# The last three output blocks of each stage run by token parts, with the next stage's first weights loaded ahead of them

## The chip, the cores and the metric

One core of a Trainium2 chip runs the whole program in one launch. The metric is the device time of one execution in microseconds (us). The core has a matrix engine (TensorE, PE in the rows), a vector engine (VectorE, DVE), an activation engine (ScalarE, ACT), GpSimd (POOL), and SyncE (SP), whose queue issues nearly all loads. Data lies in SBUF; matmuls write to eight banks of PSUM.

## The reference, cut to what matters

Two layers work on 512 latent tokens (x) and 256 context tokens (cx), of width 1024:

```
h  = rms_norm(x, norm_attn_w) * (1 + sc_m) + sh_m         # the same for cx, with its own sc and sh
u  = h @ w_in ; ya, yb, yg = three kinds of mixers of u
x  = x + g_m * (concat(ya, yb, yg) @ w_out)
hf = rms_norm(x, norm_ffn_w) * (1 + sc_f) + sh_f
x  = x + g_f * ((silu(hf @ w_gate) * (hf @ w_up)) @ w_down)
...
return rms_norm(x, final_norm_w)
```

The second layer updates no context tokens behind its mixers. What matters here is the place where one product ends and the next begins: each rms_norm needs the sum of squares over all 1024 channels of a token, thus over the outputs of all eight column blocks of the product before it, and the first matmul of the next product needs the normalised h.

## The kernel before, in words

**Layout.** x is kept with channels on the partitions, as eight blocks xT[d] of 128 channels by 768 tokens (layer 0) or 512 (behind the mixers of layer 1). A product is made block by block, d = 0 to 7: `load_w` (L341) brings the weights of one block into a raw tile `wr`, ScalarE rounds them to a high half (`wh`, L345), VectorE subtracts for the low half (`wl`, L346). `proj_ws` (L349) then makes, for each of 4, 7 or 8 blocks of the contraction, three matmuls (high by high, high by low, low by high) per token segment of at most 512 columns. `residual` (L1158) adds the block to xT[d] on VectorE (L1162), squares it on ScalarE (L1173) and adds the square to `acc` (tile MC) on VectorE (L1175).

**Rings.** Tiles of one name rotate over few buffers: `wr` has 2, `wh` and `wl` 3 each, `vh` and `vl` (a second pair for weights, used in the mixers and not in the products at stake) 2 each, and in PSUM `S` has 2 of two banks each, `PT` 2 and `sm` 2 of one bank each. A `wr` buffer is free again when both halves are made.

**The end of a stage.** `tail_blocks` (L1188) makes the last two blocks, d = 6 and 7, by token parts: 512 and 256 tokens in layer 0, twice 256 in layer 1. The order is block 6 and block 7 for part 0, block 6 for part 1, then `token_sums` (L1178) of part 0, block 7 for part 1, the spread of part 0's row, and the sums and the spread of part 1. The sums are matmuls of one column against `ones`: one group over `acc` and one over the squares of block 7. VectorE adds the two (L1207, L1208), GpSimd raises to the power of -0.5 (L286), and three small VectorE instructions refine it (L291, L292, L294). `spread` (L311) lays the row over all partitions by matmuls (L315), and ScalarE copies it from PSUM to SBUF (L320). `make_h` (L323) then makes h for each of the eight blocks d of a part: on VectorE x times scale times row (L336) or, for d = 2, 4 and 6, on ScalarE and GpSimd (L333, L334); the high half on ScalarE (L338, tiles HY and HS) and the low half on VectorE (L339, tiles HZ, PHA and PHB).

There are four such ends, called **end 1** (w_out of layer 0, 4 contraction blocks), **end 2** (w_down of layer 0, its last group of 7), **end 3** (w_out of layer 1) and **end 4** (w_down of layer 1, behind which `final`, L1260, transposes x, scales it by the row and stores it).

**The start of the next stage** uses two weight blocks at once, gate and up (L1290) or the first two of w_in (L559), and multiplies part 0 through all of h before part 1. Their loads stand behind `tail_blocks` in program order.

**Modulation.** In the feed-forward of layer 0 the generator `md` runs 56 steps of `mod_dots` (L234). Each takes one `wr` buffer, loads 512 KB into it and makes four VectorE products (L245). One or two steps are taken in the block loop, and what is left is run off ahead of end 2 (L1327).

**Order.** The program is written as one list; the order on each engine is drawn up ahead of time by a planner with estimated durations, in which the earlier entry of the list goes first where both are ready, and the engines keep to it. `issue_after` puts an instruction behind another one on its engine.

Of the kernel before, what the change touches and what calls it, by code (L numbers as in the profile page):

```python
# [14 lines left out]
P = 128  # L15
# [13 lines left out]
def hybrid_kernel(ctx: ExitStack, tc: tile.TileContext, a, out, dbg=None):  # L29
# [281 lines left out]
    def spread(rstd, n):  # L311

        pb = ps_sm()
        for tb in range(n // P):
            PE.matmul(  # L315
                pb[:, tb * P : (tb + 1) * P], lhsT=rstd[:, tb : tb + 1].to_broadcast([P, P]),
                rhs=ident, start=True, stop=True,
            )
        pbs = T(sb, "pr", 3, [P, NX])[:, 0:n]
        S.activation(pbs, pb[:, 0:n], AF.Copy)  # L320
        return pbs

    def make_h(l, xT, h, pbs, part, shi, sc):  # L323
# [3 lines left out]
        for d in range(KB):  # L327
            aside = d in (2, 4, 6)
            t1 = (mb if aside else ma)([P, NX])[:, 0:n]
            hi, lo = h[0][d][:, c0:c1], h[1][d][:, c0:c1]  # L330
            s_ = sc[d // 4][:, d % 4, v : v + 1]
            if aside:
                S.activation(t1, xT[d][:, c0:c1], AF.Copy, scale=s_)  # L333
                G.tensor_tensor(out=t1, in0=t1, in1=pbs, op=ALU.mult)  # L334
            else:
                V.scalar_tensor_tensor(t1, xT[d][:, c0:c1], s_, pbs, ALU.mult, ALU.mult)  # L336
            sh = mod_ap(l, shi, d, v)
            S.activation(hi, t1, AF.Identity, bias=sh)  # L338
            V.scalar_tensor_tensor(lo, t1, sh, hi.bitcast(F32), ALU.add, ALU.subtract)  # L339
# [176 lines left out]

    for l in range(L):
# [41 lines left out]
        ws = [wblk(i) for i in range(2)]  # L559
# [618 lines left out]
        def token_sums(src, n):  # L1178
            pq = ps_sm()
            for tb in range(n):  # L1180
                ins = PE.matmul(
                    pq[:, tb : tb + 1], lhsT=src[:, tb * P : (tb + 1) * P], rhs=ones[:, 0:1], start=True, stop=True
                )
            return pq[:, 0:n], ins.ins

        fin = False

        def tail_blocks(load, nk, xh, xl, which, order, then):  # L1188

            d0, d1 = KB - 2, KB - 1  # L1190
            ws = [load(d) for d in (d0, d1)]
            pts = [ps_s() for _ in ws]
            rs = []
            ins = None
# [6 lines left out]
            def sums(part, sq):  # L1201
                _, c0, c1 = part
                n = (c1 - c0) // P
                qa, _ = token_sums(acc[:, c0:c1], n)
                qs, ins = token_sums(sq, n)
                va, v = tiny(n), tiny(n)
                V.tensor_scalar(out=va, in0=qa, scalar1=1.0 / D, scalar2=EPS, op0=ALU.mult, op1=ALU.add)  # L1207
                V.scalar_tensor_tensor(v, qs, 1.0 / D, va, ALU.mult, ALU.add)  # L1208
                return rsqrt(v, n), ins
# [30 lines left out]
        for d in range(KB - 2):  # L1240
# [11 lines left out]

        tail_blocks(load_wo, 4, ysh, ysl_, 2, None, norm2)
# [3 lines left out]
        def load_gu(name, j):  # L1257
            return load_w(a[name][l, j].rearrange("p k c -> p (k c)"), 1024)
# [27 lines left out]
        for gi, ng in enumerate(groups):  # L1286
            gh, gl_ = [], []
            for j in range(j0, j0 + ng):
                if j == 0:
                    ws = [load_gu(n, 0) for n in ("w_gate", "w_up")]  # L1290
# [30 lines left out]
            for d in range(KB - 2 if fin else KB):  # L1321
# [97 lines left out]
```

## Time and profile before

| | |
|---|---|
| time, median of 3 runs | 1792.51 us (1790.63 to 1794.35) |
| the profiled execution: time, span | 1792.03 us, 1790.3 us |
| TensorE busy | 1735.2 us, 97% of the span |
| VectorE, ScalarE, GpSimd busy | 1025.0, 623.6, 265.6 us |
| mean granted TensorE clock | 0.986 of full |
| end 1, end 2, end 3 (about) | 482 to 515, 1040 to 1088, 1401 to 1424 us |

Times in rows are microseconds from the start of the span. A timeline's row is the start, the time from the first start to the last end, the engine, the line and the instruction, with the tile written and those read, and how many were merged (x); in brackets is the idle time of the engine ahead of it and what ended it. A merged row's time overlaps the next row's on TensorE, so lengths of matmul work are taken from start to start.

### The profile page before, as it was taken

The page shows a single profiled execution, that of the slowest core. Times are in us where ns is not written, and L with a number is a line of the kernel's source. Part 1 is how long each engine was busy: PE and PEld are TensorE (multiplying, and loading weights), DVE is VectorE, ACT ScalarE, POOL GpSimd, SP SyncE. Part 2 cuts the span into 40 slices and gives each one's busy share as a digit, 9 for nine tenths or more (in the row PEclk, how much of TensorE's full clock was granted, in tenths as well). Part 3 has the DMA queues.
Part 4 walks back from the last instruction along what each step waited for, and adds up shares of the span by engine and source line. Part 5 has one row for each costly group of instructions (what it writes and reads, how often), then busy time and mean ns, then how long its engine had stood idle before and what let it go on. Part 6 is the DMA issues. An engine that isn't in the chain of part 4 may idle for free.

```text
span 1790.3 us, 26514 instructions
## 1 busy us (share of the span) xinstructions
PE 1735.2 (97%) x10290; PEld 1472.0 (82%) x10290; DVE 1025.0 (57%) x2117; ACT 623.6 (35%) x1202; POOL 265.6 (15%) x289
## 2 busy tenths in 40 slices
PE   7999998999999999999999989999999999999998
PEld 3898886778878888888888878998777888888887
DVE  3645557985575455535554575586895743333335
ACT  4422425665352211221122234334655532232222
POOL 0103116652010000000000011222652100000000
PEclk9999998999989999999999999999999999999999
DMA  9744455522223443333343455233722233333332
GB/s 361 250 130 138 167 159 143 138 89 69 74 86 117 123 121 107 118 105 111 125 122 114 122 162 188 74 108 112 198 63 71 83 107 102 98 93 96 99 106 79
DMA packets 93742, 220.61 MB, mean 123 GB/s; under 512 B 18352, under 2 KB 26160, under 8 KB 93616
## 3 DMA queue, kind: packets, MB, share of 16 engines
q1 hardware_dynamic: 77520, 203.60, 37.3%
q10 hardware_dynamic: 16096, 15.31, 2.6%
q8 instruction: 81, 1.33, 0.3%
q14 instruction: 45, 0.37, 0.1%
HBM read 197.44 MB, written 21.43 MB: 122 GB/s over the span
## 4 chain that ended last, share of the span: by engine, by line
PE 87%; DVE 6%; DMA 3%; ACT 2%; issue 1%; POOL 1%; SPq 0%; ACTq 0%; DVEq 0%; POOLq 0%
PE S L357 66%; PE sm L371 3%; PE PT L371 3%; PE sm L459 2%; PE PT L447 2%; PE PT L357 1%; DMA wr<-in_mod_wT_dram 1%; PE S L411 1%; DVE wh L924 1%; PE S L188 1%; PE S L414 1%; PE PT L188 1%; PE PT L990 1%; PE sm L945 1%; PE sm L946 1%
## 5 line engine op out<-in xcount | busy, mean ns | idle before, releaser
L345 ACT ACTIVATE wh<-wr 128x1024 fp32r<-128x1024 f32 (+2 forms) x204 | 198.0, 972 | 742.6 <-PE S L357 567.0
L346 DVE TENSOR_TENSOR wl<-wr,wh 128x1024 fp32r<-128x1024 f32 (+2 forms) x204 | 227.9, 1118 | 186.4 <-ACT wh L345 184.1
L357 PE MATMUL S<-HY,wh 128*128 128x512 f32 (+1 forms) x716 | 215.9, 359 | 3.9 <-ACT HY L338 3.9
L357 PE MATMUL S<-HY,wl 128*128 128x512 f32 (+1 forms) x716 | 212.5, 354 | 0.3 <-DVE wl L346 0.3
L357 PE MATMUL S<-HZ,wh 128*128 128x512 f32 (+1 forms) x716 | 212.1, 354 | 0.6 <-DVE HZ L339 0.6
L357 PE MATMUL S<-HS,wh 128*128 128x512 f32 (+1 forms) x716 | 211.3, 353 | 0.0
L357 PE MATMUL S<-HS,wl 128*128 128x512 f32 (+1 forms) x716 | 209.3, 350 | 0.0
L286 POOL TENSOR_TENSOR tiny<-tiny,mhalf 128x2 f32<-128x2 f32 (+2 forms) x17 | 27.0, 1590 | 1069.6 <-DVE tiny L1208 1020.6
L245 DVE CUSTOM_DVE_ANT_0 PT<-wr,XFB 128x512 f32<-128x512 f32 x112 | 75.6, 715 | 182.8 <-DMA wr<-in_mod_wT_dram 182.8
L357 PEld LDWEIGHTS S<-HY,wh 128*128 128x128 f32 x716 | 118.7, 191 | 24.0 <-ACT HY L338 4.2
L357 PEld LDWEIGHTS S<-HZ,wh 128*128 128x128 f32 x716 | 118.7, 190 | 22.8 <-DVE HZ L339 2.1
L357 PEld LDWEIGHTS S<-HY,wl 128*128 128x128 f32 x716 | 117.8, 190 | 19.7 <-DVE wl L346 0.6
L357 PEld LDWEIGHTS S<-HS,wh 128*128 128x128 f32 x716 | 116.9, 188 | 18.1
L357 PEld LDWEIGHTS S<-HS,wl 128*128 128x128 f32 x716 | 116.2, 188 | 18.9
L357 PE MATMUL S<-PHA,wh 128*128 128x512 f32 (+1 forms) x358 | 105.6, 352 | 0.0
L357 PE MATMUL S<-PHB,wh 128*128 128x512 f32 (+1 forms) x358 | 104.7, 350 | 0.0
L357 PE MATMUL S<-GX,wh 128*128 128x512 f32 (+1 forms) x400 | 97.7, 350 | 0.4 <-DVE KA L1162 0.4
L437 POOL TENSOR_SCALAR pr<-pr,tiny 128x640 f32<-128x640 f32 (+2 forms) x80 | 72.7, 911 | 98.5 <-DVE tiny L435 89.5
L1309 DVE TENSOR_TENSOR MB<-S,MA 128x768 f32<-128x768 f32 (+1 forms) x42 | 34.6, 824 | 72.0 <-PE S L357 72.0
L357 PEld LDWEIGHTS S<-GX,wh 128*128 128x128 f32 x400 | 65.9, 189 | 11.2 <-DVE KA L1162 0.8
L447 PE MATMUL PT<-c,pr 128*128 128x128 f32 x384 | 65.4, 285 | 9.5 <-POOL pr L437 4.5
L431 ACT ACTIVATE pr<-S,tiny 128x640 f32<-128x640 f32 (+2 forms) x80 | 61.5, 770 | 32.6 <-DVE tiny L424 21.2
(436 smaller groups left out, 3670.1 us busy)
## 6 DMA issues: line engine op xcount, KB each, us to landing
wr<-in_mod_wT_dram SPq DMA_DIRECT2D x56, 512.0 KB, 3.8
wr<-in_w_gate_dram SPq DMA_DIRECT2D x44, 512.0 KB, 3.6
wr<-in_w_up_dram SPq DMA_DIRECT2D x44, 512.0 KB, 3.6
wr<-in_w_blk_dram SPq DMA_DIRECT2D x28, 512.0 KB, 3.8
wr<-in_w_down_dram SPq DMA_DIRECT2D x32, 448.0 KB, 3.4
wr<-in_w_out_dram SPq DMA_DIRECT2D x32, 256.0 KB, 2.8
wr<-in_w_down_dram SPq DMA_DIRECT2D x16, 512.0 KB, 3.5
QN<-in_mod_w_dram SPq DMA_DIRECT2D x24, 256.0 KB, 5.3
```

The lines of the kernel that those rows point to most:

```text
L188: PE.matmul(pm[32 * j : 32 * j + 32, 0:512], lhsT=cs[:, k, :], rhs=w[k], start=(k < 4), stop=(k >= 4), tile_position=(0, 32 * j),)
L245: V.tensor_tensor_reduce(out=ptile() if v == 0 else wv, in0=wv, in1=rows[2 * v + hf], scale=1.0, scalar=0.0, op0=ALU.mult, op1=ALU.add, ac ...
L286: POW.tensor_tensor(out=y, in0=v, in1=mhalf[:, 0:n], op=ALU.pow)
L345: S.activation(hi, raw, AF.Copy)
L346: V.tensor_tensor(lo, raw, hi.bitcast(F32), ALU.subtract)
L357: ins = PE.matmul(pt[:, c0:c1], lhsT=w, rhs=xx[:, c0:c1], start=(k == (0 if len(order) == 1 else order[0]) and i == 0), stop=(k == (nk - 1 ...
L371: PE.matmul(pt[:, 0:n], lhsT=s, rhs=w[:, o : o + n], start=(k == 0 and i == 0), stop=(k == KB - 1 and i == 2),)
L431: exps.append(S.activation(p_, st[:, o0:768], AF.Exp, bias=m[:, 2:3], accum_out=m[:, 3:4]).ins)
L437: G.tensor_scalar(out=p_, in0=p_, scalar1=m[:, 4:5], scalar2=1.0, op0=ALU.mult, op1=ALU.mult).ins
L447: PE.transpose(pt[:, k * P : (k + 1) * P], pr[j, qi][:, kk * P : (kk + 1) * P], ident)
L459: PE.matmul(pv[64 * j : 64 * j + 64, 0:P], lhsT=V2(kts[k], j), rhs=ph[j, qi][:, k, :], start=(k == 0), stop=(k == nkt - 1), tile_position= ...
L1309: V.tensor_tensor(gg[:, c0:c1], pu[:, c0:c1], sg[:, c0:c1], ALU.mult)
```

## The change

1. `tail_blocks` takes three blocks, d = 5, 6 and 7, in place of two. The first two use `S`, the third `PT` (and `sm` for columns from 512 on). The order is blocks 5, 6, 7 for part 0; block 5 for part 1; the sums of part 0; block 6 for part 1; the spread of part 0; block 7 for part 1; the sums and the spread of part 1. The loops ahead of it end one block earlier.
2. The first two weight blocks of the next stage are loaded ahead of the three of `tail_blocks` in program order, and are split into `vh` and `vl`: gate and up at ends 1 and 3, the first two of w_in of layer 1 at end 2. There is nothing to load ahead at end 4.
3. The two groups of sums are accumulated in one PSUM tile, in turns per 128 tokens, and one VectorE instruction (L278) takes the place of L1207 and L1208.
4. `spread` also returns the row in PSUM, and `make_h` reads that for d = 0 and 1 (both on VectorE); the other blocks read the copy.

```
...
-        return pbs
+        spread_end.append(ins.ins)
+        return pbs, pb[:, 0:n]
...
-                V.scalar_tensor_tensor(t1, xT[d][:, c0:c1], s_, pbs, ALU.mult, ALU.mult)
+                V.scalar_tensor_tensor(t1, xT[d][:, c0:c1], s_, pbs[int(d < 2)], ALU.mult, ALU.mult)
...
-        ws = [wblk(i) for i in range(2)]
+        ws = wnext or [wblk(i) for i in range(2)]
...
-            d0, d1 = KB - 2, KB - 1
-            ws = [load(d) for d in (d0, d1)]
-            pts = [ps_s() for _ in ws]
+            d0 = KB - 3
+            ws = [load(d) for d in range(d0, KB)]
+            pts = [ps_s(), ps_s(), Split()]
...
-                qa, _ = token_sums(acc[:, c0:c1], n)
-                qs, ins = token_sums(sq, n)
-                va, v = tiny(n), tiny(n)
-                V.tensor_scalar(out=va, in0=qa, scalar1=1.0 / D, scalar2=EPS, op0=ALU.mult, op1=ALU.add)
-                V.scalar_tensor_tensor(v, qs, 1.0 / D, va, ALU.mult, ALU.add)
-                return rsqrt(v, n), ins
+                pq = ps_sm()
+                for tb in range(n):
+                    for i, src in enumerate((acc[:, c0:c1], sq)):
+                        ins = PE.matmul(
+                            pq[:, tb : tb + 1], lhsT=src[:, tb * P : (tb + 1) * P], rhs=ones[:, 0:1],
+                            start=(i == 0), stop=(i == 1),
+                        )
+                return rsqrt_small(pq[:, 0:n], n, 1.0 / D), ins.ins
...
-            block(0, tparts[0])
-            _, sq = block(1, tparts[0])
-            for p0, p1 in zip(tparts, tparts[1:]):
-                block(0, p1)
-                r_, ins = sums(p0, sq)
-                with tc.issue_after(ins):
-                    ins, sq = block(1, p1)
-                with tc.issue_after(ins):
-                    row(p0, r_)
-            r_, _ = sums(tparts[-1], sq)
-            row(tparts[-1], r_)
+            p0, p1 = tparts
+            for i in range(3):
+                _, sq = block(i, p0)
+            block(0, p1)
+            r_, ins = sums(p0, sq)
+            with tc.issue_after(ins):
+                ins, _ = block(1, p1)
+            with tc.issue_after(ins):
+                row(p0, r_)
+            with tc.issue_after(ins if fin and last else spread_end[-1]):
+                _, sq = block(2, p1)
+            r_, _ = sums(p1, sq)
+            row(p1, r_)
...
-        for d in range(KB - 2):
+        for d in range(KB - 3):
             w = load_wo(d)
...
+            return load_w(a[name][l, j].rearrange("p k c -> p (k c)"), 1024, "w" if j else "v")
+
+        wgu = [load_gu(n, 0) for n in ("w_gate", "w_up")]
         tail_blocks(load_wo, 4, ysh, ysl_, 2, None, norm2)
...
-            for d in range(KB - 2 if fin else KB):
+            for d in range(KB - 3 if fin else KB):
...
+                if not last:
+                    wnext = [load_w(a["w_blk"][l + 1, i].rearrange("p k c -> p (k c)"), 1024, "v") for i in range(2)]
                 tail_blocks(load_dn, ng, gh, gl_, 5, None, final if last else lambda p_, r_: rstd.append(r_))
```

## Rows read from the trace of the kernel before

**Rows 1.** Page: busy time, share of the span and instructions by engine.

```profile
PE 1735.2 (97%) x10290; PEld 1472.0 (82%) x10290; DVE 1025.0 (57%) x2117; ACT 623.6 (35%) x1202; POOL 265.6 (15%) x289
```

**Rows 2.** TensorE's waits, whole span: total us, times, longest.

```profile
PE sm L315 <- DVE tiny L294: 4.9, 3, 2.7
PE S L357 <- ACT HY L338: 3.9, 3, 1.5
```

**Rows 3.** TensorE's timeline, end 1.

```profile
482.01 0.62 PE L357 MATMUL S<-GX,wh 128*128 128x512 f32 x2
...
487.46 0.40 PE L357 MATMUL S<-GX,wh 128*128 128x256 f32 x2
...
488.89 0.95 PE L1181 MATMUL sm<-ones,MC 128*128 128x1 f32 x8
...
490.59 0.48 PE L357 MATMUL S<-GX,wh 128*128 128x256 f32 x2
...
494.92 1.37 PE L315 MATMUL sm<-c,tiny 128*128 128x128 f32 x8 [2.65 <-DVE tiny L294]
...
514.47 0.28 PE L357 MATMUL S<-HY,wh 128*128 128x256 f32 x1
```

**Rows 4.** TensorE: timeline; by stretch: length, busy (matmuls), granted clock, DMA share, GB/s.

```profile
42.00 1.86 PE L200 MATMUL S<-c,SA 128*128 128x2 f32 x8 [3.08 <-DVE SA L194]
...
42.00:43.00 1.00, 1.00 (x5) 0.50 1.02 409
...
500.00:502.00 2.00, 2.00 (x5) 0.50 0.00 0
```

**Rows 5.** VectorE's timeline, then GpSimd's, end 1.

```profile
487.66 0.75 DVE L1162 SCALAR_TENSOR_TENSOR QN<-S,mod,QN 128x512 f32<-128x512 f32 x1 [0.19 <-PE S L357]
490.12 1.23 DVE L346 TENSOR_TENSOR wl<-wr,wh 128x1024 fp32r<-128x1024 f32 x1
491.60 0.15 DVE L1208 SCALAR_TENSOR_TENSOR tiny<-sm,tiny 128x4 f32<-128x4 f32 x1
497.05 1.82 DVE L336 SCALAR_TENSOR_TENSOR MA<-KA,sc,pr 128x512 f32<-128x512 f32 x1
517.08 0.48 DVE L339 SCALAR_TENSOR_TENSOR PHB<-MA,mod,HS 128x256 fp32r<-128x256 f32 x1
...
491.89 1.01 POOL L286 TENSOR_TENSOR tiny<-tiny,mhalf 128x4 f32<-128x4 f32 x1 [68.87 <-DVE tiny L1208]
```

**Rows 6.** The chain of work through end 2, in order of time.

```profile
1023.16 4.30 DMA wr<-in_mod_wT_dram
...
1052.63 0.96 ACT wh L345
```

**Rows 7.** SyncE's queue ahead of end 2: blocks 5, 6 and an `md` load.

```profile
1021.11 0.33 SPq L343 DMA_DIRECT2D wr<-in_w_down_dram  x1
1030.09 0.33 SPq L240 DMA_DIRECT2D wr<-in_mod_wT_dram  x1
1044.60 0.33 SPq L343 DMA_DIRECT2D wr<-in_w_down_dram  x1
```

**Rows 8.** TensorE's timeline, end 2.

```profile
1040.41 0.87 PE L357 MATMUL S<-GV,wh 128*128 128x512 f32 x4
...
1087.77 0.28 PE L357 MATMUL S<-HY,wh 128*128 128x256 f32 x1
```

**Rows 9.** End 3: SyncE's queue, then TensorE's timeline.

```profile
1394.17 0.93 SPq L343 DMA_DIRECT2D wr<-in_w_out_dram  x2
...
1401.24 0.62 PE L357 MATMUL S<-GX,wh 128*128 128x512 f32 x2
...
1424.04 0.28 PE L357 MATMUL S<-HY,wh 128*128 128x256 f32 x1
```

**Rows 10.** Page: loads, their KB and median us from issue to landing.

```profile
wr<-in_w_gate_dram SPq DMA_DIRECT2D x44, 512.0 KB, 3.6
...
wr<-in_w_out_dram SPq DMA_DIRECT2D x32, 256.0 KB, 2.8
```

More of the change, by code (lines that the diff above doesn't have):

```diff
@@ L314, in spread @@
         for tb in range(n // P):
-            PE.matmul(
+            ins = PE.matmul(
                 pb[:, tb * P : (tb + 1) * P], lhsT=rstd[:, tb : tb + 1].to_broadcast([P, P]),
@@ L320, in spread @@
         S.activation(pbs, pb[:, 0:n], AF.Copy)
-        return pbs
+        spread_end.append(ins.ins)
+        return pbs, pb[:, 0:n]
+    spread_end = []
     def make_h(l, xT, h, pbs, part, shi, sc):
@@ L333, in make_h @@
                 S.activation(t1, xT[d][:, c0:c1], AF.Copy, scale=s_)
-                G.tensor_tensor(out=t1, in0=t1, in1=pbs, op=ALU.mult)
+                G.tensor_tensor(out=t1, in0=t1, in1=pbs[0], op=ALU.mult)
             else:
-                V.scalar_tensor_tensor(t1, xT[d][:, c0:c1], s_, pbs, ALU.mult, ALU.mult)
+                V.scalar_tensor_tensor(t1, xT[d][:, c0:c1], s_, pbs[int(d < 2)], ALU.mult, ALU.mult)
             sh = mod_ap(l, shi, d, v)
@@ L515, in hybrid_kernel @@
     mod_chunk(0, 3, mw[1])
+    wnext = None
     for l in range(L):
@@ L1176, in residual @@
             return sq
[L1178 to L1184, printed above, removed]
         fin = False
         def tail_blocks(load, nk, xh, xl, which, order, then):
-            d0, d1 = KB - 2, KB - 1
-            ws = [load(d) for d in (d0, d1)]
-            pts = [ps_s() for _ in ws]
+            d0 = KB - 3
+            ws = [load(d) for d in range(d0, KB)]
+            pts = [ps_s(), ps_s(), Split()]
             rs = []
-            ins = None
             def block(i, part):
@@ L1203, in sums @@
                 n = (c1 - c0) // P
-                qa, _ = token_sums(acc[:, c0:c1], n)
-                qs, ins = token_sums(sq, n)
-                va, v = tiny(n), tiny(n)
-                V.tensor_scalar(out=va, in0=qa, scalar1=1.0 / D, scalar2=EPS, op0=ALU.mult, op1=ALU.add)
-                V.scalar_tensor_tensor(v, qs, 1.0 / D, va, ALU.mult, ALU.add)
-                return rsqrt(v, n), ins
+                pq = ps_sm()
+                for tb in range(n):
+                    for i, src in enumerate((acc[:, c0:c1], sq)):
+                        ins = PE.matmul(
+                            pq[:, tb : tb + 1], lhsT=src[:, tb * P : (tb + 1) * P], rhs=ones[:, 0:1],
+                            start=(i == 0), stop=(i == 1),
+                        )
+                return rsqrt_small(pq[:, 0:n], n, 1.0 / D), ins.ins
             def row(part, r_):
                 rs.append(r_ if fin and last else spread(r_, part[2] - part[1]))
-            block(0, tparts[0])
-            _, sq = block(1, tparts[0])
-            for p0, p1 in zip(tparts, tparts[1:]):
-                block(0, p1)
-                r_, ins = sums(p0, sq)
-                with tc.issue_after(ins):
-                    ins, sq = block(1, p1)
-                with tc.issue_after(ins):
-                    row(p0, r_)
-            r_, _ = sums(tparts[-1], sq)
-            row(tparts[-1], r_)
+            p0, p1 = tparts
[11 more added lines that the diff above has]
+            row(p1, r_)
             for part, r_ in zip(tparts, rs):
@@ L1251, in norm2, with load_gu @@
             make_h(l, xT, hs2, r_, part, 3, sc2)
+        def load_gu(name, j):
+            return load_w(a[name][l, j].rearrange("p k c -> p (k c)"), 1024, "w" if j else "v")
+        wgu = [load_gu(n, 0) for n in ("w_gate", "w_up")]
         tail_blocks(load_wo, 4, ysh, ysl_, 2, None, norm2)
         hh, hl = hs2
-        def load_gu(name, j):
-            return load_w(a[name][l, j].rearrange("p k c -> p (k c)"), 1024)
         def final(part, r_):
@@ L1289, in hybrid_kernel @@
                 if j == 0:
-                    ws = [load_gu(n, 0) for n in ("w_gate", "w_up")]
+                    ws = wgu
                     pg, pu = ps_s(), Split()
```

## The prediction

> **What bounds the kernel now.** I read the busy times first: TensorE works 97% of the span and no other engine over 57% [rows 1], so an edit pays only if TensorE waits less, or runs faster, somewhere. The waits of TensorE come next: the two that belong to the ends of stages are the spread, which waits for the refined row, and the first matmul on a new h [rows 2]. They sum to 8.8 us in three places. The timelines of the ends show that this is only half of it: behind the waits the granted clock is 0.50 of full [rows 4], 1.2 in place of 2.4 GHz, for some 6 us of good work. So I price each end by what it takes against what its matmuls take at full clock.
>
> At end 1, twelve matmuls of 512 columns take (487.46 - 482.01) / 2 = 2.73 us, twelve of 256 take 1.43, part 0's sums 1.70 [rows 3]. From 482.01 to the first h matmul of part 1 at 514.47 are 32.5 us. The work in it is 2 x 2.73 + 2 x 1.43 + 1.70, then spreads and part 1's sums (about 2.5, an estimate from start to start), then 48 h matmuls at 2.73 / 12 = 0.227 (10.9): 23.4. **Lost: 9.1 us.**
>
> At end 2 I count from the start of block 5: 47.4 us [rows 8]. A block is 21 matmuls per part, 21/12 of the above (4.77 and 2.50 us), so the work is 3 x 7.27 + 1.7 + 2.5 + 10.9 = 36.9. **Lost: 10.5 us**, some 2.6 of it ahead of blocks 6 and 7, where TensorE waits for weights: the chain of work goes there through an `md` load and the split of block 7's weights [rows 6].
>
> At end 3 block 5 starts at 1401.24; with 2.73 for it, 4 x 1.43, half the sums and spreads of end 1 (2.4) and 48 h matmuls at 0.12 (5.7), the work is 16.6 of 22.8 us [rows 9]. **Lost: 6.2 us.** At end 4 nothing follows but a chain of small steps.
>
> **The change part by part.**
>
> *The new order and the early splits (gain).* The spread of part 0 starts 494.92 - 490.59 = 4.3 us after the last of its sums was issued [rows 3]. In between, a split of 1.23 us stands ahead of L1208, and another of that kind ahead of L292 [rows 5]. Without them the chain is 0.2 + 0.16 for the one instruction from PSUM, 0.1 + 1.01 on GpSimd and three times 0.2: 2.1 us. Block 6 of part 1 covers 1.43 of it at ends 1 and 3 and 2.50, all of it, at end 2. Left is 0.7, or 1.1 with a residual in the way; I take 0.9. Were a split to slip in again (those of the second pair of weights become ready about then, when `wh` comes free), it would be 1.2 more; the range keeps that.
>
> Then block 7 of part 1 covers the first h. Its chain from the end of the spread is the copy 0.6, VectorE's first product, the high half 0.7 and 0.3 of hops. The product waits now: it takes 1.82 us beside a GpSimd product (L334), where an instruction of the same kind with one operand in PSUM takes 0.75 [rows 5]. I take the latter, its nearest row; the bounds are 0.75 and 1.82. So h comes 2.35 us behind the spread, 0.9 behind the block at end 1, at once at end 2, and 0.2 late at end 3 with 256 columns.
>
> The Trainium skill (SBUF — State Buffer, "Who interferes with whom") states that a VectorE instruction with two SBUF inputs shuts out, or is shut out by, a GpSimd instruction that reads SBUF, and one with a single SBUF input does not. The trace agrees as far as it goes, 1.82 against 0.75; by the rule the row in PSUM ends that wait, and without it h would come 1.1 us later at end 1. A rule of the same skill speaks against the edit (PSUM — Partial Sum Buffer, "PSUM bank collisions raise a hardware error"): two engines may not be in one bank at once, so the product must not start beside ScalarE's copy of the row. No row here shows such a pair; were the two allowed together, h would come 0.6 us sooner.
>
> VectorE sets another bound. From its first product at 497.05 to its last low half at 517.56 it is busy with h for 20.5 us [rows 5]. The half clock gave it time. At full clock TensorE wants both parts in 10.9 + 5.7 us and a spread, so it will catch up with VectorE; I take 0.8 us at ends 1 and 2 (0 to 3), and nothing at end 3, where the following block's matmuls fill in. With 0.5 for the squares ahead of part 0's sums and 0.4 for a one in seven chance of half clock, **end 1 then loses 3.5 us (2 to 6): 5.6 saved.**
>
> *The loads ahead (cost).* Every weight passes through the two `wr` buffers, and SyncE's queue takes them in program order: block 5 at 1021.11, then the last five `md` loads, then block 6 at 1044.60, though TensorE stood waiting for it [rows 7]. So what is put ahead of blocks 5, 6 and 7 makes these late, unless there is slack.
>
> At end 1 there is: a block lasts 4.2 us, its transfer is 2.8 [rows 10], and block 5's weights are split two blocks ahead. Two loads of 3.6 with splits of about 1 and 1.23 in two buffers take some 6 us, about 4 of which that lead and the freed buffer absorb. No cost; if the lead fails, 2 us.
>
> At end 2 there is none. Block 5's load loses its place ahead of the five `md` loads and gets the two new ones ahead of it as well: seven loads from 1021.11 on. Four in the same ring took 1044.60 - 1030.09 = 14.5 us, 3.6 each [rows 7]. I take 3.5, as the last two need a split and not four products. (Bounds: 3.1, half of a median transfer of 3.6 and 2.6 of products; 4.15, half of a 4.30 transfer [rows 6], products and a residual.) Block 5 is issued at 1021.1 + 24.5 = 1045.6, lands 3.6 later and has its high half after another 0.96: 1050.2. TensorE is ready for it at 1040.41: **it idles 9.8 us (7.0 to 14.6)**, and no other work is in reach. One idle stretch of 3.1 us ahead of 42.0 already ended in half clock [rows 4], so I add 3 us for six at 0.50. With 0.8 for VectorE, end 2 loses 13.6 (10 to 18) against 10.5: **3.1 dearer.** That the waits at blocks 6 and 7 and at the spread go is counted in.
>
> At end 3 the buffers come free at 1394.17 and 1394.8 for blocks 5 and 6 [rows 9]. Now gate and up go there. They land after about 4.2 (two at once), are split by 1400.9 and 1402.5 with the residuals between, and only then block 5 is loaded: 1400.9 + 2.8 + 0.63 = 1404.3, against 1401.24. That is 3.1 us, 0.5 more for the low half and 0.6 for blocks 6 and 7; bounds 1.5 (transfers not slowed by each other, splits at once) and 6. Half clock behind it I price at 1.7 (two chances in three of 2.5). With 0.9 at the spread, 0.2 at h and 0.2 for block 5 in 256-column pieces, end 3 loses 7.2 (3 to 11) against 6.2: **1.0 dearer.**
>
> *End 4.* Block 5 in pieces costs 21 x (2 x 0.119 - 0.227) = 0.2 us. Behind the last squares six matmuls are left in place of four: 0.2. L1207 was hidden, so its removal is worth nothing. Transposes have one `PT` bank less: 0 to 0.6. **0.5 dearer (0 to 1).** The first h of the program reads PSUM too; TensorE waits there for modulation, so nothing.
>
> **The sum** is made against the profiled execution, 1792.03 us (0.5 below the median of the runs): -5.6 + 3.1 + 1.0 + 0.5 = -1.0, **1791.0 us**. What this kernel's measurement can tell is 0.2%, 3.6 us; so I forecast no change that can be told.
>
> **The rivals.**
> *A. The loads have slack.* If `wr` does not hold blocks 5 to 7 up, end 2 keeps only 2 us of its 10.5 and end 3 two of its 6.2: 1792.0 - 5.6 - 8.5 - 4.2 + 0.5 = 1774. Against it stand rows 6 and 7: TensorE waited for block 6 with fewer loads ahead.
> *B. The ring is quicker than I price it.* At 3.1 us a load end 2 idles 7.0, and at end 3 the stall is 1.5 and the clock stays full: 2.8 + 4.4 less, 1783.8 us. It needs the transfers at their medians, and the splits at once.
> *C. The ring is slower, so the kernel is slower.* At 4.15 us a load block 5 comes 4.8 us later at end 2: 1795.8, over the bound from 4.1 us a load on; with end 3's transfers slowed likewise (stall of 6 us in place of 4.2), 1797.6. For it: one `md` transfer took 4.30 with the queue full [rows 6].
> *D. VectorE sets the pace.* If TensorE gets h no sooner, as VectorE is 20.5 us at it, end 1 saves 3 and end 2 pays 2 more: 1795.6. It lies at the edge.
>
> **How the numbers follow.** No change that can be told (1788.4 to 1795.6, with the mild forms of B and D): 0.42. A: 0.09. B and what else ends below 1788.4: 0.22. C, with D on top: 0.27. So faster 0.31, same 0.42, slower 0.27. Likeliest is 1791; its own range is 1788 to 1796. The range of 8 in 10 reaches to B and C, 1783 to 1798; A and the worst of C are left out.
>
> **What would show it.** Right: at end 2 one idle of 7 us or more ahead of block 5's first matmul, ended by L345, with a granted clock of 0.50 behind it; at end 3 one of 2 to 5 us; in SyncE's queue two w_in loads between the last `md` load and block 5's. At end 1 waits under 1.2 us ahead of the spread and of h, and a clock of 1.00 through all h matmuls; its first L336 near 0.75. Wrong: block 5's weights split by 1041 at end 2, or a clock that still falls at end 1.

## The result and the profile after: 0.8% slower

The changed kernel takes 1806.2 us (median of four runs, 1802.8 to 1808.2), the kernel before on the same chip 1791.6. The ratio is 1.0077, with a 95% interval of 1.0057 to 1.0097: slower, where I forecast no change that can be told (1791.0) and a range up to 1798. The profiled execution of the changed kernel is its quickest, 1802.8 us with a span of 1801.0; that of the kernel before has 1790.3.

Which of TensorE's waits are longest now (engine and line, who ended the wait, sum in us, times, longest), with lines of the matmul helper 3 higher (L357 is L360, the weight's high half L345 is L348, the low half of h L339 is L342):

```profile
PE S L360 <- ACT wh L348: 12.3, 3, 9.4
...
PE S L360 <- DVE HZ L342: 4.4, 3, 1.8
...
PE sm L315 <- DVE tiny L294: 3.0, 2, 2.4
PE S L360 <- ACT HY L341: 2.5, 2, 1.5
PE sm L1202 <- ACT MB L1177: 1.8, 2, 1.6
```

The waits of [rows 2] fell from 4.9 and 3.9 us to 3.0 and 2.5, as the change means them to. Beside them stand three that were small or not there: for the weights of a block (1.0 us before), for low halves of h, and for squares.

**End 2.** TensorE's timeline and SyncE's queue, which answer to [rows 8] and [rows 7], then the clock by stretch (length, busy times of TensorE, its weight loads, VectorE, ScalarE and GpSimd, granted clock, DMA share, GB/s):

```profile
1034.58 0.51 PE L360 MATMUL S<-GK,wl 128*128 128x512 f32 x2
1044.53 1.22 PE L360 MATMUL S<-GV,wh 128*128 128x512 f32 x2 [9.43 <-ACT wh L348]
```

```profile
1026.22 3.76 SPq L240 DMA_DIRECT2D wr<-in_mod_wT_dram  x2
1032.34 0.33 SPq L571 DMA_DIRECT2D xsp<-KB  x1
1033.96 3.68 SPq L346 DMA_DIRECT2D wr<-in_w_blk_dram  x2
1039.83 0.33 SPq L346 DMA_DIRECT2D wr<-in_w_down_dram  x1
```

```profile
1044.00:1048.00 4.00, 3.47 (x8) 2.37 (x9) 1.48 (x3) 1.43 (x2) 0.00 (x0) 0.50 0.67 207
...
1080.00:1084.00 4.00, 3.73 (x10) 2.98 (x11) 4.00 (x7) 3.05 (x5) 1.76 (x1) 0.61 0.00 0
```

TensorE is ready for block 5 at 1035.1 and gets it at 1044.53. In the queue the last `md` loads and the two `w_in` loads stand ahead of block 5's load at 1039.83. TensorE ran dry, and the first matmuls behind the idle run at half clock. The second stretch lies where h is made, and there VectorE is busy all the time (4.00 of 4.00 us). That is not new: the kernel before runs at 0.50 from 1074 to 1079 us, and VectorE is busy for the whole of it.

**End 1.** VectorE's timeline, which answers to [rows 5], and the clock:

```profile
485.92 1.23 DVE L349 TENSOR_TENSOR wl<-wr,wh 128x1024 fp32r<-128x1024 f32 x1 [0.22 <-ACT wh L348]
487.06 0.15 DVE L294 SCALAR_TENSOR_TENSOR tiny<-tiny,tiny 128x4 f32<-128x4 f32 x1
...
489.16 1.41 DVE L339 SCALAR_TENSOR_TENSOR MA<-KA,sc,sm 128x512 f32<-128x512 f32 x2 [1.60 <-ACT pr L320]
...
491.64 1.22 DVE L349 TENSOR_TENSOR wl<-wr,wh 128x1024 fp32r<-128x1024 f32 x1
...
493.45 1.76 DVE L342 SCALAR_TENSOR_TENSOR HZ<-MA,mod,HY 128x512 fp32r<-128x512 f32 x1
```

```profile
492.00:496.00 4.00, 2.63 (x15) 2.23 (x14) 3.99 (x5) 3.16 (x6) 2.08 (x2) 1.00 0.45 131
496.00:500.00 4.00, 2.81 (x7) 1.76 (x7) 3.35 (x6) 1.33 (x4) 2.23 (x3) 0.51 0.00 0
500.00:504.00 4.00, 4.00 (x15) 3.30 (x15) 3.45 (x5) 2.11 (x5) 1.32 (x1) 0.64 0.00 0
```

The first pair is split already, but a split of 1.23 us still stands ahead of the row's last step (L294): it is the next pair's, let in early. The two products from PSUM take 0.7 us each, as forecast. A low half behind them takes 1.76 us, while GpSimd's first product runs (493.22, 1.43 us), and TensorE waits for it. At 496 the clock falls, as it did before; a clock that still falls at end 1 was one of my signs of being wrong.

**Where the time went.** For each instruction that two kernels have in common I took the difference of its start in the two traces, and the median of it in a stretch between two ends; the change of this median over an end is what the end costs more than in the kernel before. In us:

| kernel | ahead of end 1 | end 1 | feed-forward, layer 0 | end 2 | mixers, layer 1 | end 3 | rest | sum |
|---|---|---|---|---|---|---|---|---|
| changed kernel | -6.0 | +0.5 | 0 | +8.1 | +0.2 | +8.0 | 0 | +10.8 |
| early loads alone | -4.5 | +0.1 | 0 | +9.8 | +1.8 | +5.7 | 0 | +12.9 |
| tail alone | -4.1 | -1.4 | 0 | +3.7 | +0.9 | +0.9 | -0.3 | -0.3 |
| PSUM read alone | -5.1 | -0.2 | 0 | -1.2 | +1.3 | -0.1 | 0 | -5.3 |
| without early loads | -2.0 | -1.1 | 0 | -2.9 | +5.4 | -0.1 | 0 | -0.7 |
| that, no low halves | -4.4 | -3.4 | 0 | 0 | +2.2 | -0.3 | 0 | -5.9 |
| loads behind | -4.4 | +0.3 | 0 | +2.7 | +1.9 | +5.5 | -0.1 | +5.9 |
| VectorE's splits held | -3.0 | -0.6 | -7.9 | +2.3 | +1.8 | +7.7 | -0.1 | +0.2 |
| ScalarE's splits held | -3.1 | -2.7 | -7.5 | +5.3 | +3.1 | +2.5 | -0.1 | -2.5 |
| md steps moved | -2.7 | -1.0 | +2.6 | +0.6 | +1.7 | +6.5 | 0 | +7.7 |

The 6 us ahead of end 1 are not the change's: all kernels of the table have 2 to 6 there, also the one whose TensorE instructions are those of the kernel before (PSUM read alone). The profiled execution of before happened to run three stretches at half clock there, at 28, 42 and 205 us, which an execution of the other kernel did not; the medians of the two kernels agree. That is a part of it only: four other profiles have these stretches too and still stand some 3 us ahead. The mixers of layer 1, where the edits touch the first two weights at most, scatter likewise, from +0.2 to +5.4; the +5.4 comes with two stretches of half clock, at 1250 and 1277 us, that the kernel before does not have. An end is surer: in the two profiles whose end 3 runs the code of the kernel before (`md` steps moved on it, narrow matmul first; both below) it differs by 0.3 and 0.6 us. So the long columns are sure to some 5 us and an end to about 1; ends 2 and 3 stand far above that. With `md` steps moved, TensorE falls behind in the last blocks ahead of end 2, and how much counts for the blocks hangs on where the stretch ends: by its starts just ahead of end 2 the last row has +4.9 and -1.7. The sum of these two columns is the same either way.

### The profile page after: what moved, and what is told of

Read it like the earlier page. It is cut to its first block, busy times and chain, and to the rows that moved or that the text cites. A ratio compares the mean times of both kernels' runs of the same rounds, so it can differ in the third digit from the quotient of the medians.

```text
span 1801.0 us, 26576 instructions
## 1 busy us (share of the span) xinstructions
PE 1736.6 (96%) x10323; PEld 1473.9 (82%) x10323; DVE 1022.7 (57%) x2115; ACT 622.6 (35%) x1206; POOL 261.9 (15%) x289
## 4 chain that ended last, share of the span: by engine, by line
PE 83%; DVE 8%; DMA 3%; ACT 2%; issue 1%; POOL 1%; ACTq 0%; SPq 0%; DVEq 0%; POOLq 0%
PE S L360 63%; PE PT L374 3%; PE sm L374 3%; PE sm L462 2%; PE PT L360 2%; DMA wr<-in_mod_wT_dram 2%; PE PT L450 1%; DVE wh L928 1%; PE S L414 1%; DVE wl L349 1%; PE S L188 1%; PE PT L188 1%; ACT wh L348 1%; PE S L417 1%; PE PT L994 1%
## 5 line engine op out<-in xcount | busy, mean ns | idle before, releaser
L348 ACT ACTIVATE wh<-wr 128x1024 fp32r<-128x1024 f32 (+2 forms) x198 | 191.7, 969 | 752.9 <-PE S L360 566.1
L349 DVE TENSOR_TENSOR wl<-wr,wh 128x1024 fp32r<-128x1024 f32 (+2 forms) x198 | 222.4, 1124 | 196.5 <-ACT wh L348 193.2
L360 PE MATMUL S<-HY,wh 128*128 128x512 f32 (+1 forms) x696 | 206.8, 356 | 0.3 <-ACT wh L348 0.3
L360 PE MATMUL S<-HY,wl 128*128 128x512 f32 (+1 forms) x696 | 204.9, 353 | 0.3 <-DVE wl L349 0.3
L360 PE MATMUL S<-HS,wh 128*128 128x512 f32 (+1 forms) x696 | 204.8, 354 | 0.0
L360 PE MATMUL S<-HZ,wh 128*128 128x512 f32 (+1 forms) x696 | 203.5, 352 | 0.0
L360 PE MATMUL S<-HS,wl 128*128 128x512 f32 (+1 forms) x696 | 202.8, 351 | 0.0
L360 PEld LDWEIGHTS S<-HZ,wh 128*128 128x128 f32 x696 | 113.8, 189 | 20.4 <-DVE MA L339 0.8
L360 PEld LDWEIGHTS S<-HY,wh 128*128 128x128 f32 x696 | 113.4, 189 | 19.6 <-issue 1.7
L360 PEld LDWEIGHTS S<-HY,wl 128*128 128x128 f32 x696 | 112.9, 188 | 19.2 <-DVE wl L349 0.6
L360 PEld LDWEIGHTS S<-HS,wl 128*128 128x128 f32 x696 | 112.4, 188 | 18.7
L360 PEld LDWEIGHTS S<-HS,wh 128*128 128x128 f32 x696 | 113.0, 188 | 17.9
L360 PE MATMUL S<-PHA,wh 128*128 128x512 f32 x348 | 102.3, 352 | 0.0
L360 PE MATMUL S<-PHB,wh 128*128 128x512 f32 x348 | 101.4, 351 | 0.0
L360 PE MATMUL S<-GX,wh 128*128 128x512 f32 (+1 forms) x376 | 93.6, 355 | 2.9 <-ACT wh L348 2.5
L360 PEld LDWEIGHTS S<-GX,wh 128*128 128x128 f32 x376 | 63.3, 193 | 13.5 <-ACT wh L348 2.9
```

Source lines behind the costliest of these rows:

```text
L348: S.activation(hi, raw, AF.Copy)
L349: V.tensor_tensor(lo, raw, hi.bitcast(F32), ALU.subtract)
L360: ins = PE.matmul(pt[:, c0:c1], lhsT=w, rhs=xx[:, c0:c1], start=(k == (0 if len(order) == 1 else order[0]) and i == 0), stop=(k == (nk - 1 ...
```

## The experiments

Each was timed beside the kernel before (its median was 1790.0 to 1791.4 us in the four groups of runs); intervals are 95%.

### The parts by themselves

**Early loads alone**, on the kernel before, whose tail stays at two blocks:

```diff
+        wgu = [load_gu(n, 0) for n in ("w_gate", "w_up")]      # into vh, vl
         tail_blocks(load_wo, 4, ysh, ysl_, 2, None, norm2)
...
+                    wnext = [load_w(a["w_blk"][l + 1, i]..., 1024, "v") for i in range(2)]
                 tail_blocks(load_dn, ng, gh, gl_, 5, None, ...)
```

> The kernel before with the early loads alone: w_gate and w_up of block 0, and the next layer's first two w_in weights, are loaded into vh and vl ahead of the last two blocks; the tail stays at two blocks. Theory R: at end 2 block 6 waits for two more loads (some 7 us), at end 3 some 2 us, half clock behind both: 1800 us or more. Theory V: the loads cost little by themselves, 1793 us or less.

1805.2 us, ratio 1.0090 (1.0075 to 1.0105). Theory R. The early loads alone cost what the whole change costs, at ends 2 and 3, and nothing at end 1.

**The tail of three blocks alone**, with separate sums and the row in SBUF:

```diff
-            d0, d1 = KB - 2, KB - 1
+            d0 = KB - 3
...
+            for i in range(3):
+                _, sq = block(i, p0)
+            block(0, p1)
```

> The kernel before with the tail of three blocks alone: blocks 5 to 7 by parts, in the order of the changed kernel; the next stage's weights are loaded where they were, the token sums stay in two banks, h reads the row in SBUF. Theory R: no load stands ahead of block 5, so nothing is lost at ends 2 and 3 and the later spread costs little: 1790 us (1787 to 1793). Theory V (the new order lets TensorE catch up with VectorE, so waits for h and half clock take what the order gains): 1795 us or more, with waits ended by L339 or by the low halves at each end.

1793.0 us, 1.0019 (1.0007 to 1.0030): the upper edge of theory R, with the waits of theory V. At end 1 no stretch of half clock is left (the kernel before has 10.2 us of it from 495.6 on), yet the end gains 1.4 us alone: TensorE's waits for low halves (3.0) and for the spread (2.9) took the place of the slow clock. End 2 is 3.7 dearer. There block 5's load, which stood ahead of the last five `md` loads [rows 7], now stands behind them with the others, and TensorE waits 3.7 us for it.

**The PSUM read alone:**

```diff
-                V.scalar_tensor_tensor(t1, xT[d][:, c0:c1], s_, pbs, ALU.mult, ALU.mult)
+                V.scalar_tensor_tensor(t1, xT[d][:, c0:c1], s_, pbs[int(d < 2)], ALU.mult, ALU.mult)
```

> The kernel before with one edit: the first two products of make_h read the row in PSUM. TensorE's and SyncE's order is that of the kernel before. Theory P (the 6 us that the changed kernel gained ahead of end 1 come from this read, through the first h of the program): 1786 us. Rival (they come from the order that the planner found): no change, 1791 us, and TensorE's half clock at 42 to 49 us and at 206 to 209 us stays.

1791.1 us, 1.0000 (0.9988 to 1.0013): nothing. At end 1 the read does what it should, and it is lost behind it; GpSimd, VectorE and ScalarE:

```profile
492.02 1.27 POOL L334 TENSOR_TENSOR MB<-MB,pr 128x512 f32<-128x512 f32 x1 [4.31 <-ACT pr L320]
492.01 1.40 DVE L336 SCALAR_TENSOR_TENSOR MA<-KA,sc,sm 128x512 f32<-128x512 f32 x2
493.32 0.72 ACT L333 ACTIVATE MB<-QN,sc 128x512 f32<-128x512 f32 x1 [1.37 <-PE sm L1181]
493.95 1.32 ACT L338 ACTIVATE HY<-MA,mod 128x512 fp32r<-128x512 f32 x2
```

Beside a GpSimd product two products take 1.40 us, where one took 1.82 before [rows 5]. But ScalarE makes the first high half behind an instruction for GpSimd (L333), which waits 1.37 us for TensorE's sums. So the high half starts 2.60 us behind the start of the copy of the row (491.35), as in the kernel before (2.61).

Theory P is out by the median, though this profile shows the 5 us. The clock by stretch of the kernel before, then of this one, shows where these come from:

```profile
42.00:46.00 4.00, 4.00 (x15) 3.59 (x15) 4.00 (x9) 2.99 (x4) 0.00 (x0) 0.50 1.00 402
...
204.00:208.00 4.00, 4.00 (x27) 4.00 (x26) 3.16 (x8) 1.46 (x3) 0.00 (x0) 0.69 1.04 367
```

```profile
42.00:46.00 4.00, 3.70 (x17) 3.00 (x18) 4.00 (x9) 2.37 (x4) 0.46 (x1) 1.00 1.03 414
...
204.00:208.00 4.00, 4.00 (x33) 3.87 (x33) 2.33 (x8) 1.90 (x3) 0.43 (x1) 1.00 1.01 347
```

**The changed kernel without the early loads**, the other three parts as they are:

```diff
-        wgu = [load_gu(n, 0) for n in ("w_gate", "w_up")]
         tail_blocks(load_wo, 4, ysh, ysl_, 2, None, norm2)
...
-                    ws = wgu
+                    ws = [load_gu(n, 0) for n in ("w_gate", "w_up")]
...
-        ws = wnext or [wblk(i) for i in range(2)]
+        ws = [wblk(i) for i in range(2)]
```

> The changed kernel without the early loads: tail of three blocks, token sums in one bank, first products of h from PSUM; the next stage's first weights are loaded where they were. Theory E (the early loads alone make the kernel slower, and the other three parts are worth nothing together): 1793 us, as with the tail alone. Rival (sums in one bank and the PSUM read shorten the row and the first h): 1790 us or less, with waits ahead of the spread and of the first h shorter than those of the tail alone (2.9 us and 0.5 us at end 1).

1791.4 us, 1.0007 (0.9995 to 1.0020). Theory E: of the 14.6 us all but one are the early loads', and what the other parts bring together can't be told from nothing.

### What the loads hold up at end 2

**The early loads behind the blocks' loads:**

```diff
             ws = [load(d) for d in range(d0, KB)]
+            nxt = ahead() if ahead else None     # the next stage's two weights
```

> The changed kernel, but with the next stage's two weights loaded behind the last three blocks' weights in the program (still into vh and vl, still ahead of the blocks' matmuls). Theory R (the wr ring: the loads put ahead of blocks 5 to 7 make these late): the idle of 9.4 us ahead of block 5 at end 2 and of 2.5 us at end 3 go, with the half clock behind them; some 12 us less than the changed kernel's 1806.2, 1794 us. Theory V (VectorE hands out h and its own work sets the pace whatever stands in the ring): the idles only move to the first h matmuls, about 1802 us.

1798.6 us, 1.0055 (1.0040 to 1.0070). Half of it: end 2 falls from +8.1 to +2.7, the idle from 9.4 to 3.6 us. End 3 keeps 5.5 of its 8.0, though its loads are no longer in the way.

**The md steps moved ahead, the early loads left where they are:**

```diff
-                step_md(j % 2 if j > 1 else 0)
+                step_md(1 if j in (10, 12, 16, 18, 20) else j % 2 if j > 1 else 0)
```

> The changed kernel with one edit: five steps of the modulation products are taken in up blocks 10, 12, 16, 18 and 20, so that no md load is left ahead of block 5 at end 2. The two w_in loads still stand ahead of it. Theory R (seven loads of some 3.5 us in the ring made the idle of 9.4 us): with two in place of seven the idle falls below 2 us and the half clock behind it goes: 1795 us (1793 to 1798). Rival (the two w_in loads alone hold block 5 up, or the md products cost as much in the blocks they move to): 1803 us or more.

1799.4 us, 1.0061 (1.0046 to 1.0076). TensorE's waits of this kernel at end 2:

```profile
PE S L360 <- DVE HZ L342: 1.8, 1, 1.8
PE S L360 <- ACT HY L341: 1.5, 1, 1.5
PE S L360 <- DVE KB L1166: 1.2, 1, 1.2
PE sm L315 <- DVE tiny L294: 0.6, 1, 0.6
```

The wait for the weight is gone, and end 2 costs 0.6 in place of 8.1. So the seven loads made the idle: the two alone do no harm, the five alone cost the 3.6 us of the run before. That the time fell less than forecast is the products' price: TensorE now waits 1.8 us at the `w_down` blocks for the high half of the gated product, and the feed-forward blocks are 2.6 dearer.

**The same on the kernel before, and in three mixtures.** In up blocks from 9 on (six steps), on the kernel before:

> The kernel before with one edit: from block 9 on, each up block of layer 0 takes a step of the modulation products too, so that none of the md loads is left to stand between the last blocks' weights. Theory R (at end 2 what stands in the wr ring ahead of a block is what TensorE waits for): the 2.4 us of waits for blocks 6 and 7 and the half clock behind them go, 1786 us. Rival (VectorE and the h chain of end 2 take it back, or the md products only disturb the blocks before): no change, 1790 us.

1795.3 us, 1.0022 (1.0010 to 1.0035): by TensorE's starts just ahead of end 2 and behind it, end 2 gains 4.4 and the blocks pay 8.0. Without early loads, with five steps placed as above:

> A version that might beat both kernels: the changed kernel without the early loads and with the five md steps moved into up blocks 10, 12, 16, 18 and 20 (not into the last up block of a group, whose product the down blocks wait for). If the waits at end 2 go and the products find room: 1788 us. If the products cost what the waits did: 1791.5 us, as without the move.

1791.8 us, 1.0004 (0.9993 to 1.0015): end 2 gains 4.3, the blocks pay 4.2. The second does what its rival said, and the first is dearer than its rival: in the blocks TensorE now waits for the gated product (some 5 and 4 us), so the products cost there at least what they cost at end 2. Two more mixtures, below, say the same.

### Is it VectorE that sets the pace behind the spread?

The changed kernel without early loads, and without the low halves of h in the feed-forward stage (the matmuls read the high half twice):

```diff
-            V.scalar_tensor_tensor(lo, t1, sh, hi.bitcast(F32), ALU.add, ALU.subtract)
+            if h[0] is not h[1]:
+                V.scalar_tensor_tensor(lo, t1, sh, hi.bitcast(F32), ALU.add, ALU.subtract)
...
```

> The changed kernel without the early loads, and with the low halves of the h of the feed-forward stage left out: VectorE makes none, and the matmuls that read a low half read the high half instead, so TensorE's work is the same. Theory V (at ends 1 and 3 VectorE's work on h sets TensorE's pace): the waits for low halves go and no others take their place, some 4 us at end 1 and 2 at end 3 less than the same kernel with them, 1787 us. Rival (the row's chain and the clock set the end, VectorE has slack): within 1 us of it, 1792 us.

1784.8 us, 0.9969 (0.9956 to 0.9982), 6.6 below the same kernel with them. The stretch of end 1 where h is made, without the low halves and with them:

```profile
500.00:510.00 10.00, 10.00 (x59) 8.83 (x58) 2.75 (x6) 7.32 (x18) 3.00 (x4) 1.00 0.31 107
```

```profile
500.00:510.00 10.00, 8.20 (x39) 6.40 (x38) 9.24 (x13) 5.99 (x11) 6.15 (x5) 1.00 0.01 2
```

With them VectorE is busy 9.24 of 10 us and TensorE runs 39 matmuls; without, TensorE is busy all the time and runs 59, some of them narrower, as it is further on. Theory V holds at end 1, where 2.3 us more go. At end 3 the table shows no gain beyond its scatter, so the 4 and 2 us that I expected are not borne out place by place, and where the rest of the 6.6 comes from stays open.

### What else holds end 3

**VectorE's splits held**, on top of the loads behind the blocks:

```diff
-                    w = load_gu("w_gate", j)
+                    with tc.issue_after(refined[-1]):        # the row of part 1
+                        w = load_gu("w_gate", j)
...
```

> The changed kernel with the early loads behind the last three blocks' weights, and VectorE's share of splitting the weights of feed-forward blocks 1 and later held until the row of part 1 is refined. Theory S (at end 3 it is the splits of the second pair of weights, let in early because the first pair is already done, that hold up the token sums in VectorE's queue): the waits of 2.4 us for the accumulated squares and 1.9 us ahead of the spread go at end 3, 1794 us. Rival (something else holds them, such as the splits of the first pair): no change, 1798.5 us.

1792.7 us, 1.0016 (1.0004 to 1.0028). The time is what theory S forecast, and yet it fell: end 3 costs 7.7 us, and the wait ahead of the sums is 2.6. The gain is in the feed-forward blocks (last section). ScalarE's timeline at end 3 shows what the theory missed:

```profile
1396.72 1.06 ACT L350 ACTIVATE vh<-wr 128x1024 fp32r<-128x1024 f32 x1 [1.18 <-DMA wr<-in_w_gate_dram]
1397.69 0.40 ACT L1179 ACTIVATE MB<-QN 128x256 f32<-128x256 f32 x1
1399.29 1.06 ACT L350 ACTIVATE vh<-wr 128x1024 fp32r<-128x1024 f32 x1 [1.20 <-DMA wr<-in_w_up_dram]
1400.26 0.71 ACT L1179 ACTIVATE MB<-QN 128x256 f32<-128x256 f32 x2
1402.58 1.06 ACT L350 ACTIVATE wh<-wr 128x1024 fp32r<-128x1024 f32 x1 [1.62 <-DMA wr<-in_w_gate_dram]
1403.55 0.40 ACT L1179 ACTIVATE MB<-QN 128x256 f32<-128x256 f32 x1
```

Each square of the tail stands behind a split that waits for its transfer. TensorE was done with the blocks that it had at 1399.8 and began the sums at 1402.39. VectorE's half of the same splits, which this hold leaves where it was, is in the way as well: the square that the sums wait for is done at 1400.7, and VectorE adds it to `acc` at 1401.92, behind a low half.

```profile
1400.38 1.23 DVE L351 TENSOR_TENSOR vl<-wr,vh 128x1024 fp32r<-128x1024 f32 x1 [0.22 <-ACT vh L350]
1401.53 0.48 DVE L1168 SCALAR_TENSOR_TENSOR QN<-S,mod,QN 128x256 f32<-128x256 f32 x1
1401.92 0.42 DVE L1181 TENSOR_TENSOR MC<-MC,MB 128x256 f32<-128x256 f32 x1
```

**ScalarE's splits held**, until the squares of part 0 are issued, and those of the second pair until the last square:

```diff
             for i in range(3):
                 _, sq = block(i, p0)
+            with tc.issue_after(squares[-1]):
+                nxt = ahead() if ahead else None
             block(0, p1)
...
```

> The changed kernel with the next stage's two weights loaded behind the last three blocks' weights, as in the run that did this alone, and with ScalarE's share of splitting them held until the squares of part 0 are issued (the share of the pairs after them until the last square). Theory Q (ScalarE takes its instructions in order; a split that waits for its transfer stands ahead of the squares, so the token sums and all behind them come late): the waits ahead of the sums at end 3 (2.4 us) and the half clock behind them go, some 5 us less than without the hold, 1793.5 us. Rival (VectorE's splits or the ring do it): no change, 1798 us or more.

1788.8 us, 0.9990 (0.9980 to 1.0001): the quickest kernel here that leaves nothing out, though not surely quicker than the kernel before. At end 3 no wait for squares is left, the clock is 1.00 from 1385 to 1425 us, and the end costs 2.5 in place of 5.5. So theory Q holds for 3 us, with one limit: a low half needs its high half, so the hold moved VectorE's splits of the first pair too (to 1403.15, behind the sums), and how much of the 3 us is ScalarE's queue and how much VectorE's was not separated. The spread now waits 2.7 us for the row. The other 7 us below the run with loads behind come mostly from the feed-forward blocks again, and end 2 costs 5.3 here.

With five `md` steps moved as well (up blocks 2, 4, 16, 18 and 20):

> The changed kernel with the early loads behind the last three blocks' weights and the splits held for the squares (1788.8 us), and five md steps moved into up blocks 2, 4, 16, 18 and 20, away from blocks 10 to 14. Theory R (at end 2 the md loads are what is left to wait for: 5.0 us ahead of block 5): the wait goes and the products find room: 1783 us. Rival (they cost in the feed-forward blocks what they cost at end 2): 1788 us.

1794.1 us, 1.0008 (0.9990 to 1.0025). The wait of 5.0 us is gone, and by TensorE's starts end 2 gains 6.8 us on the run without the move; the feed-forward blocks give back 6.0 and the mixers of layer 1 1.6. End 1 is the same in both. The rival, and dearer than it put it.

### The pace of pairs

**Narrow matmul first**, on the kernel before:

```diff
-                    proj_ws(pg, w[0], w[1], hh, hl, KB, osegs)
+                    proj_ws(pg, w[0], w[1], hh, hl, KB, osegs[::-1])
...
```

> The kernel before with one edit: in the feed-forward blocks of layer 0 from block 1 on, each pair of matmuls with the same weight takes its 256 columns first and its 512 columns second. TensorE's work is the same. In the traces a pair takes either 0.353 us or 0.347 us for hundreds of us on end. Theory P (which of the two it is hangs on how the stream of pairs starts, so another start can give the quick one): up to 10 us less than the kernel before, 1780 us, if it falls on the quick pace, and 1790 us if it falls on the slow one; a pace between them speaks against it.

1791.6 us, 1.0010 (1.0000 to 1.0020): the slow pace. **The hold of VectorE's splits on the kernel before**, and on the changed kernel without early loads:

> The kernel before with one edit: VectorE's share of splitting the weights of feed-forward blocks 1 and later is held until the row of part 1 is refined, as in the run that did this on top of the early loads. Theory P (the hold changes how the stream of pairs of matmuls starts in block 1 of layer 0, and that start sets a pace of 0.347 in place of 0.353 us a pair up to end 2): some 7 us less than the kernel before, 1783 us, with the quick pace from about 525 us on. Rival (what the hold gave came from end 3, or from another part of the changed kernel): no change, 1790 us.

> The changed kernel without the early loads, and with the same hold. Theory P: 1784 us, the quick pace in layer 0. Rival: 1791 us, as without the hold.

1790.3 us, 1.0003 (0.9989 to 1.0016), and 1791.0, 1.0002 (0.9988 to 1.0017). Both keep the slow pace; theory P is out in that form: the hold does not set it by itself. Hold and moved `md` steps on the kernel before:

> A version that might beat both kernels: the kernel before with the hold and with four md steps moved into up blocks 4, 16, 18 and 20. If the hold gives the quick pace and end 2 loses its waits: 1780 us. If only one of the two does: 1784 us. If neither: 1790 us.

1796.0 us, 1.0028 (1.0013 to 1.0044): neither. Counted in the same way, the products cost 10.8 us in the blocks here, and end 2 gains 4.

## Why the prediction was wrong, step by step

**The loads ahead, end 2: mechanism and idle right.** Forecast was an idle of 9.8 us ahead of block 5, for seven loads in the ring; it is 9.4, and without the `md` loads it is gone. Rival A (slack) is out. But the end costs 8.1 us more, not 3.1. The term that was mis-sized is "0.8 for VectorE", for what comes after the idle: there TensorE waits 0.65 for the spread, 1.5 for the high half and 1.8 for the low half of h, and then runs 3.4 us at half clock once more, some 5.7 in all. (At 4.15 us a load the idle adds up to 14.3 us, not 14.6, and rival C to 1795.6; nothing hangs on it.)

**The loads ahead, end 3: too small by 7.** The stall ahead of block 5 is 2.5 + 0.2 us (forecast 3.1 + 0.5). TensorE's waits from 1380 to 1450 us in the changed kernel:

```profile
PE S L360 <- ACT wh L348: 2.5, 1, 2.5
PE sm L1202 <- ACT MB L1177: 1.8, 2, 1.6
PE S L360 <- ACT HY L341: 1.0, 1, 1.0
```

What the step left out stands behind it: the splits that the early loads bring into the tail take ScalarE's and VectorE's turns there. The squares come late, TensorE waits 1.6 us for them and 1.0 for h, and the clock falls three times. Two holds show that it is the splits of the first pair, on ScalarE and behind it on VectorE, for 3 us of the 5.5 that are left with the loads behind the blocks; the rest of end 3 was not settled.

**The new order and the early splits, end 1: failed.** Forecast was a gain of 5.6 us; the changed kernel loses 0.5 there, and the tail alone gains 1.4. Three statements under it were wrong. Splits would leave the row's chain: the next pair's came in their place, as I had named and left to the range (the spread waits 2.4, forecast 0.9). VectorE's work on h would cost 0.8: it sets the pace, and taking the low halves away frees 2.3 us. It had no slack in the kernel before either, where it is busy for 8.00 of 8 us (the third of the busy times) while TensorE runs mostly at half clock:

```profile
500.00:508.00 8.00, 8.00 (x23) 5.96 (x24) 8.00 (x13) 4.97 (x9) 3.47 (x3) 0.63 0.00 0
```

And the lost 9.1 us that I counted at end 1 were taken for a stock to draw on, with half of it in the slow clock. A slow clock under a late h cost next to nothing of its own here: the tail alone has the full clock there, and waits instead. This was rival D's mechanism, which I priced too low and put against ends 1 and 2 alone.

**The PSUM read: worth nothing, and not what shortened the product.** The product takes 0.7 us in place of 1.82, and I put that down to its operand in PSUM. But the tail alone, with the row in SBUF, has the same:

```profile
491.31 1.41 DVE L339 SCALAR_TENSOR_TENSOR MA<-KA,sc,pr 128x512 f32<-128x512 f32 x2 [2.00 <-ACT pr L320]
```

In the new order GpSimd's first product comes 4.1 us later than VectorE's, so nothing stands beside it, and h follows the row as soon without the read as with it: the first high half starts 1.42 us behind the start of the copy in both kernels. The step that failed is that I took the GpSimd product that stands beside VectorE's in the kernel before to stand beside it in the new order too; "without it h would come 1.1 us later" has no run for it. The trace of the PSUM read alone agrees with the rule of the Trainium skill (SBUF — State Buffer, "Who interferes with whom"): two products with a single operand in SBUF take 1.40 us beside a GpSimd product. A wait that I did not price came with the read: TensorE's sums of part 1 wait 0.9 us at end 1 for the second product (L339) of part 0. That the read keeps the row's bank from the next user until then fits the ring of two `sm` buffers, and was not tested.

**End 4** was forecast at +0.5 and shows nothing. **Rival C** ended on the right side for another reason: the ring is not slower than I priced it, the tails behind it are. My chances name C with D on top, but no case of mine summed the ring as I priced it with h chains that are late at all three ends, which is what came: +8.1, +8.0 and +0.5.

## What to carry to other kernels

A load put ahead for the next stage is paid in every queue that it passes: here in the ring of raw buffers behind other loads, in ScalarE's queue ahead of squares, and in VectorE's, ahead of the sums of squares, where the freed buffer then lets yet another pair in. A reading of who stands beside whom holds for the order that it was read in; after a change of order it has to be read again. Before counting idle time and slow clock at an end as gain, ask which engine would set the pace if both were gone; here VectorE's work on h took nearly all of it back. And compare a profile with a second one of the same program first: the kernel before with its `md` steps moved, whose instructions are the same up to 726 us, stood 4.8 us ahead by end 1.

## What the runs showed of the hardware beside that

In the feed-forward blocks of layer 0 each weight serves 512 and 256 columns in turn. The same pairs run at one of two paces, for hundreds of us, both at granted clock 1.00. By stretch, the changed kernel, then the one with ScalarE's splits held:

```profile
700.00:750.00 50.00, 50.00 (x285) 43.38 (x284) 24.10 (x52) 10.16 (x11) 0.00 (x0) 1.00 0.38 116
```

```profile
700.00:750.00 50.00, 50.00 (x291) 44.10 (x290) 24.19 (x57) 10.16 (x11) 0.00 (x0) 1.00 0.36 114
```

TensorE is busy throughout and runs 285 or 291 matmuls in 50 us, 2% apart. The timelines of the kernel before and of the one with VectorE's splits held show the pairs; in the slow pace each third takes 0.36 us, in the quick one all take some 0.347:

```profile
800.15 0.51 PE L357 MATMUL S<-HZ,wh 128*128 128x512 f32 x2
800.50 0.51 PE L357 MATMUL S<-HY,wl 128*128 128x512 f32 x2
800.85 0.53 PE L357 MATMUL S<-HY,wh 128*128 128x512 f32 x2
801.21 0.51 PE L357 MATMUL S<-HZ,wh 128*128 128x512 f32 x2
```

```profile
800.31 0.51 PE L362 MATMUL S<-HY,wh 128*128 128x512 f32 x2
800.66 0.51 PE L362 MATMUL S<-HZ,wh 128*128 128x512 f32 x2
801.00 0.51 PE L362 MATMUL S<-HY,wl 128*128 128x512 f32 x2
801.35 0.51 PE L362 MATMUL S<-HY,wh 128*128 128x512 f32 x2
```

The quick pace began at about 520 us, at the start of block 1, in the profiles of the three kernels that hold splits and have early loads. In two it lasts and is worth 7.5 to 8 us up to end 2; the third falls back to the slow pace between 900 and 960 us, in blocks with moved `md` steps. Two other profiles change to the quick one late, behind waits. That it hangs on how the stream starts is argued, not shown: neither the hold nor the order of the columns alone gave it.
